# Two of four block sums by accumulating DMA, rows and activations parked in DRAM, and weight splitting ordered operation by operation, in an encoder layer

## The chip, the core and the metric

The kernel runs on one core of a Trainium2 chip. The metric is device time in microseconds; the profile is one execution of the program. TensorE multiplies, VectorE (DVE) and ScalarE (ACT) do the elementwise work, GpSimd (POOL) and SyncE (SP) issue the DMAs.

## What is computed

One encoder layer on 256 tokens of width 2048 in float32. The parts that matter here (constants filled in):

```python
h = layer_norm(x)
proj = h @ w_in                              # 2048 x 6144
...                                          # neighbourhood and differential attention
mixed = concat(na_out, diff_out) @ w_out     # 2048 x 2048
h = layer_norm(2**0.25 * h + mixed)
ffn = (silu(h @ w_gate) * (h @ w_up)) @ w_down   # 2048 x 5632 twice, 5632 x 2048
out = layer_norm(2**0.25 * h + ffn)
```

## The kernel before

**Products in three passes.** A float32 operand is split into a high part, rounded to the float32r type by a ScalarE copy (`split_hi`, line 336), and a low part, the difference, by a VectorE subtraction (`split_lo`, line 340). A product is three matmuls into one PSUM bank: high x high, high x low, low x high. Weights come as units of 128 rows by 1024 columns (`load`, line 326, on SP's queue) into the slab, a pool of 46 tiles of 4 KB for each partition, which also holds transposed activations and everything else of that size. Tokens are two tiles of 128.

**The units in order** (lines 307 to 322): six groups of the input projection, two of the output projection, the last 512 columns of gate and up together, ten groups of gate (`g`) and up (`u`) of 1024 columns each in turn, two groups of the down projection (`d`). Each group runs over its k tiles of 128 rows.

**Seven products.** In the `g` and `u` groups two neighbouring k tiles, two token tiles and two column halves make a 2 x 2 block product. `products` (line 931) lists seven products of 128 x 512 for four pairs of k tiles of a group (`SEVEN`, the pairs 0, 2, 4, 6) and eight for the four others. A seven pair needs sums of weight blocks. With r1 and r2 the two units, and columns in halves a and b, `seven_parts` (line 891) makes on VectorE: t1 = r1a + r1b and t3 = r1b + r2b in one tile, t2 = t1 + r2b and t4 = t2 + r2a in another; each tile is split as a whole, r1a by itself, and r2 as an ordinary unit. The products of sums 1 and 3 are the fourth and fifth, those of sums 2 and 4 the sixth and seventh. At a group's end VectorE joins the PSUM banks (`block_end`, line 1011); after a `u` group four tiles of middle activations are transposed on TensorE and copied to the slab by ScalarE (`mid_side`, line 866), where eleven tiles stay until the down projection; `mid_split` (line 874) splits them there. The residual rows `h` (four slab tiles) stay from the start to the end.

**The order of the queues.** The program is written out by a planner. `Timed` (line 60) keeps a clock for each engine and one for DMA from cost formulas (`note`, line 93) and when each tile is ready. The loop at line 1254 goes through the steps; a step in the `g` and `u` groups is one product. At each step it writes what must be there:

```python
window = order[i : i + (AHEAD_S if step.kind == "product" else AHEAD)]
for s in window[:URGENT]:          # URGENT = 3
    s.finish_parts()               # all that is left of these steps' weight work
```

then, up to eight times, elementwise side work, weight work of the steps in the window that the planner's clocks find ready while the clocks of ScalarE and VectorE are at most `SPARE` (2 us) ahead of TensorE's, and side work on TensorE. `finish_parts` (line 1223) writes a pair's whole list, and all products of a pair have that list. The engines then take their own instructions strictly in the written order. `Step.load` (line 1210) asks for weights `NPRE_S` units ahead. The planner's formulas used below:

```python
LATENCY = dict(pe=0.2, act=0.15, dve=0.13, pool=0.1, dma=1.2)              # line 61
start = self.clock[name] = max(self.clock[name], start) + (1.05 if name == "pool" else 0.1)
end = max(self.clock["dma"], start) + float(max(rows * dims[-1] * 4 / 360e3, rows * 0.0026))
if name == "pool": end += 2.0                                              # lines 102 to 105
cost = m / 2400 + 0.0135      # a matmul          (117)
cost = 0.1 + n / 1200         # ScalarE           (119)
cost = 0.07 + n / 960         # VectorE, two inputs (122)
```

Of the kernel before, what the change touches and what calls it, by code (L numbers as in the profile page):

```python
# [35 lines left out]
NSG = 5  # L36
SEVEN = (0, 2, 4, 6)


class Engine:  # L40
# [6 lines left out]
    def __getattr__(self, op):  # L47
        def call(*args, **kw):
            result = getattr(self.engine, op)(*args, **kw)  # L49
            outs, ins = [], []  # L50
            for i, (key, x) in enumerate([("", x) for x in args] + list(kw.items())):
                if hasattr(x, "tensor") and hasattr(x, "ap"):
                    (outs if key in ("out", "accum_out") or (i == 0 and not key) else ins).append(x)
            self.timed.note(self.name, op, outs, ins)
            return result

        return call
# [187 lines left out]
def layer_kernel(ctx: ExitStack, tc: tile.TileContext, A: dict, out: bass.AP):  # L245
# [6 lines left out]
    slab = ctx.enter_context(tc.tile_pool(name="slab", bufs=46))  # L252
# [8 lines left out]

    def slot(shape, dt=F32):
        return slab.tile(shape, dt, tag="slab", name=nm("sl"))
# [61 lines left out]

    def load(u):
        if u >= U:
            return
        r = slot([P, 1024])
# [14 lines left out]
    def split(u):  # L344
        if u not in wh:
            split_hi(u)
            split_lo(u)

    acc = {}

    def mm_step(t, u):
# [5 lines left out]
        xh = xh[:, t * P : (t + 1) * P]  # L357
        xl = xl[:, t * P : (t + 1) * P]
# [7 lines left out]
        nc.tensor.matmul(a1, xl, hi[:, 512:], start=False, stop=sp)  # L366

# [21 lines left out]
    AHEAD_S = 13  # L389
    NPRE = 7  # L390
    NPRE_S = 5
# [55 lines left out]
    def ln_side(key, t, g, b, store, tiles, n_whole):  # L447
# [10 lines left out]
        for c in range(4):  # L458
# [6 lines left out]
            if key == "1":  # L465
                if c not in hF:
# [39 lines left out]
    hF, forms = {}, {}  # L506

    def more_forms(i):
# [17 lines left out]
        parts = slot([P, 2, n, P], F32R)  # L526
# [339 lines left out]
    def mid_side(c, t, m):  # L866
        yield "pe", [m]
        bk = pe_transpose4(m)
        if c not in mid_whole:
            mid_whole[c] = slot([P, 4, S])  # L870
        nc.scalar.copy(mid_whole[c][:, :, t * P : (t + 1) * P], bk.rearrange("p (a b) -> p a b", b=P))
        have["mid whole", c] = have.get(("mid whole", c), 0) + 1

    def mid_split(c):

        if c not in mid_tiles:
            side.drain_until(lambda: have.get(("mid whole", c), 0) == 2)
            new_T(mid, mid_tiles, c)
            hi, lo = mid_tiles[c]
            nc.scalar.activation(hi, mid_whole[c], AF.Copy)  # L880
            nc.vector.tensor_tensor(lo, mid_whole[c], hi.bitcast(F32), op=ALU.subtract)
            have["mid", c, 0] = have["mid", c, 1] = 1
# [48 lines left out]
    def products(u):  # L931
# [13 lines left out]
        def t(n, m):  # L945
            return lambda: (sums[u]["hi"][n][:, m], sums[u]["lo"][n][:, m])

        a_, b_, c_, d_ = x(0, 0), x(1, 0), x(0, 1), x(1, 1)
        if i in SEVEN:
            def b11():  # L950
# [6 lines left out]
                (5, f(3), t(0, 0)),  # L957
                (7, f(0), t(0, 1)),
                (6, f(1), t(1, 0)),
                (4, d_, t(1, 1)),  # L960
# [14 lines left out]
    def take_product(u, n):  # L975
# [11 lines left out]
        nc.tensor.matmul(q[m], xl, yh, start=False, stop=stop)  # L987
        if not any(x in left for x in (1, 6, 7)) and 1 in q:
# [4 lines left out]
            nc.vector.tensor_tensor(vw[:, 0], q[7], e[:, 1], op=ALU.add)  # L993
            part["q1"], part["v"], part["vw"], part["w"] = e[:, 0], e[:, 1], vw[:, 0], vw[:, 1]
# [12 lines left out]
        elif stop and m == 4:  # L1007
            block_end(name, 1, 0, q[4], part["vw"], ALU.subtract)
            banks.give(q.pop(4))
# [311 lines left out]
```

## Time and profile before

| | us |
|---|---|
| median of 3 runs | 1149.44 (1146.36 to 1149.57) |
| the profiled execution | 1151.8 |
| its span, first to last instruction | 1150.0 |
| TensorE busy in the span | 1128.6 (98%) |
| VectorE busy | 855.2 (74%) |
| ScalarE busy | 572.3 (50%) |
| GpSimd busy | 43.2 (4%) |

Busy times are averages over stages with different limits, and a busy TensorE is not TensorE at its peak, since matmuls are pipelined: the number of matmuls in a stretch says more. All instructions carry the line of one helper (L49), so groups are told apart by the program's names: `sl` is a slab tile, `acc` a PSUM bank, `s`, `o` and `nb` are small rings of tiles. "a <-b" in a wait names the one that ended it. PEclk and the column behind the engines are the granted clock of TensorE as a share of full speed.

### The profile page before, as it was taken

To read this page: it belongs to the slowest core of one execution; us is meant where nothing else is said; L and a number is where in the kernel's file an instruction comes from. 1 tells how busy PE (TensorE), PEld (TensorE's weight loads), DVE (VectorE), ACT (ScalarE), POOL (GpSimd) and SP (SyncE) were. 2 spreads that over 40 slices of the span, in tenths; PEclk is the share of its full clock that TensorE was granted. 3 is DMA by queue.
4 is the path that set the end of the run, shared out by engine and by line. 5 is a ranking of instruction groups with operands and counts; after the bars stand their busy time and mean duration, and the time that the engine had idled before them with its cause. 6 is when DMAs were issued, how large, how long until landed. Compare 5 with 4: busy or idle time off the path is not lost.

```text
span 1150.0 us, 13909 instructions
## 1 busy us (share of the span) xinstructions
PE 1128.6 (98%) x5064; PEld 914.2 (79%) x5064; DVE 855.2 (74%) x1110; ACT 572.3 (50%) x740; POOL 43.2 (4%) x81
## 2 busy tenths in 40 slices
PE   9999999999999999999999999999999999999997
PEld 4788888888888858888778778778778888888885
DVE  7863866447784399989999989999989855455535
ACT  5552655426572155654654654555556544434420
POOL 2000002111000000000000000000000000000001
PEclk9999999999999999999999999999999999999999
DMA  9864548796676623656555556465556755577621
GB/s 329 268 187 151 154 148 184 189 216 157 163 255 204 235 91 115 213 187 203 195 185 196 170 188 234 128 220 183 170 196 223 269 194 174 177 232 246 217 79 73
DMA packets 64053, 218.51 MB, mean 190 GB/s; under 512 B 7669, under 2 KB 7797, under 8 KB 63985
## 3 DMA queue, kind: packets, MB, share of 16 engines
q1 hardware_dynamic: 61056, 209.74, 54.3%
q0 software_dynamic: 2768, 7.81, 5.0%
q8 instruction: 39, 0.64, 0.2%
q14 instruction: 30, 0.24, 0.1%
q10 hardware_dynamic: 160, 0.08, 0.0%
HBM read 215.50 MB, written 2.11 MB: 189 GB/s over the span
## 4 chain that ended last, share of the span: by engine, by line
PE 78%; DVE 13%; issue 3%; ACT 3%; DMA 1%; POOL 1%; POOLq 0%; ACTq 0%; DVEq 0%
PE acc L49 78%; DVE sl L49 10%; ACT sl L49 3%; DVE s L49 1%; DVE o L49 1%; ACT s L49 0%; DMA ident<-in_c_ident_dram 0%; DMA sl<-in_w_gate_dram 0%; DMA sl<-in_w_up_dram 0%; DVE stats L49 0%; POOL rstd L49 0%; POOL rs L49 0%; ACT o L49 0%; ACT L49 0%; POOLq L1317 0%
## 5 line engine op out<-in xcount | busy, mean ns | idle before, releaser
L49 PE MATMUL acc<-sl,sl 128*128 128x512 f32 (+1 forms) x4712 | 1076.7, 389 | 12.2 <-DVE o L49 5.5
L49 PEld LDWEIGHTS acc<-sl,sl 128*128 128x128 f32 x4712 | 869.5, 189 | 200.5 <-DVE sl L49 10.8
L49 DVE TENSOR_TENSOR sl<-sl,sl 128x1024 fp32r<-128x1024 f32 (+2 forms) x611 | 628.7, 1073 | 124.9 <-ACT sl L49 96.6
L49 ACT ACTIVATE sl<-sl 128x1024 fp32r<-128x1024 f32 (+1 forms) x491 | 473.2, 1011 | 297.1 <-DVE sl L49 167.5
L49 ACT ACTIVATE sl<-acc 128x256 fp32r<-128x256 f32 (+2 forms) x70 | 33.0, 499 | 102.4 <-PE acc L49 89.7
L49 DVE TENSOR_TENSOR sl<-acc,sl 128x256 fp32r<-128x256 f32 (+2 forms) x92 | 53.2, 593 | 33.4 <-ACT sl L49 32.6
L49 ACT COPY sl<-acc 128x512 f32<-128x512 f32 x50 | 28.2, 586 | 77.5 <-PE acc L49 77.4
L49 DVE SCALAR_TENSOR_TENSOR sl<-sl,acc 128x512 f32<-128x512 f32 x16 | 10.9, 679 | 58.1 <-PE acc L49 58.1
L49 DVE TENSOR_SCALAR sl<-acc 128x512 f32<-128x512 f32 x8 | 5.5, 688 | 37.2 <-PE acc L49 37.2
L49 DVE TENSOR_TENSOR sl<-sl 128x512 f32<-128x512 f32 x40 | 27.3, 683 | 0.0
L49 POOL DMA_DIRECT2D sl<-in_ln_g_dram x4 | 2.2, 560 | 652.2 <-DMA sl<-in_w_down_dram 596.7
L49 POOL DMA_DIRECT2D nb<-in_na_rpb_dram x32 | 19.6, 620 | 87.5 <-DVE s L49 87.5
L49 ACT ACTIVATE s<-s 128x512 f32<-128x512 f32 x20 | 12.3, 633 | 20.6 <-DVE s L49 20.6
L49 ACT ACTIVATE s<-s,mx 128x256 f32<-128x256 f32 x32 | 15.9, 500 | 12.5 <-DVE mx L49 12.5
L49 PEld LDWEIGHTS acc<-ident,s 128*128 128x128 f32 x136 | 17.1, 145 | 4.7 <-DVE o L49 0.9
L49 PE MATMUL acc<-ident,s 128*128 128x128 f32 x136 | 20.7, 281 | 0.1
L49 PEld LDWEIGHTS acc<-ident,sl 128*128 128x128 f32 x128 | 15.0, 140 | 7.0 <-issue 3.2
L49 DVE SCALAR_TENSOR_TENSOR sl<-sl,rstd,sl 128x512 f32<-128x512 f32 x22 | 16.5, 751 | 4.0 <-POOL rstd L49 3.1
L49 DVE BATCH_NORM_STATS2 stats<-sl 128x6 f32<-128x512 f32 x24 | 16.3, 690 | 3.0 <-DMA sl<-in_x_dram 2.4
L49 DVE SCALAR_TENSOR_TENSOR sl<-sl,mv,sl 128x512 f32<-128x512 f32 x24 | 17.7, 746 | 0.3
L49 PE MATMUL acc<-ident,sl 128*128 128x128 f32 x128 | 17.6, 273 | 0.1
L49 ACT ACTIVATE rows<-ident,rstd 128x128 f32<-128x128 f32 x1 | 0.4, 402 | 34.3 <-POOL rstd L49 34.3
(74 smaller groups left out, 198.9 us busy)
## 6 DMA issues: line engine op xcount, KB each, us to landing
sl<-in_w_in_dram SPq DMA_DIRECT2D x96, 512.0 KB, 4.9
sl<-in_w_down_dram SPq DMA_DIRECT2D x88, 512.0 KB, 4.3
sl<-in_w_gate_dram SPq DMA_DIRECT2D x80, 512.0 KB, 4.0
sl<-in_w_up_dram SPq DMA_DIRECT2D x80, 512.0 KB, 4.3
sl<-in_w_out_dram SPq DMA_DIRECT2D x32, 512.0 KB, 5.4
sl<-in_w_gate_dram SPq DMA_DIRECT2D x16, 256.0 KB, 4.0
sl<-in_w_up_dram SPq DMA_DIRECT2D x16, 256.0 KB, 4.2
sl<-in_x_dram SPq DMA_DIRECT2D x8, 256.0 KB, 5.0
```

Source lines behind the costliest of these rows:

```text
L49: result = getattr(self.engine, op)(*args, **kw)
```

## The change

- In a seven pair, sums 2 and 4 are made in the tile of sum 1, by two GpSimd DMAs that add a half of r2 from its slab tile (`accum_op`). Sum 2 is split before the second DMA. Sums 1 and 3 are made and split as before; sums 2 and 4 are split one by one into a tile each.
- The weight work is a list of single operations, each with its engine, what it reads and which of the list must come before (`op`, `seven_parts`, `one_parts`); `next_part` takes the first that is ready by the planner's clocks and whose engine's clock is at most `SPARE` ahead. `finish_parts` and `URGENT` are as before.
- The normalized residual rows go to DRAM after their transposes (eight GpSimd DMAs) and come back by four SP DMAs in the down projection's first group. The middle activations go to DRAM from a ring of two tiles (22 GpSimd DMAs) and come back one tile of four k tiles at a time (11 SP DMAs). Two of the sums' operand tiles for eight pairs share one slab tile.
- The planner is told which slab tiles are free (`leave`, `follows`). The window of steps `AHEAD_S` goes from 13 to 20, the weights asked for ahead, `NPRE_S`, from 5 to 8 units.

The diff, cut:

```diff
+    slots = dict(used=0, left=[])
     def slot(shape, dt=F32):
-        return slab.tile(shape, dt, tag="slab", name=nm("sl"))
+        t = slab.tile(shape, dt, tag="slab", name=nm("sl"))
+        if slots["used"] < SLOTS:
+            slots["used"] += 1
+        elif slots["left"]:
+            old = min(slots["left"], key=lambda x: nc.idle(x))
+            slots["left"].remove(old)
+            nc.follows(t, old)
+        return t
+    def leave(*tiles):
+        slots["left"] += tiles
     rings = {}
...
     raw, wh, wl = {}, {}, {}
+    h_d = dram.tile([2 * P, D], F32, name="h_d")
+    mid_d = dram.tile([NFC * P, 1024], F32, name="mid_d")
     def load(u):
         if u >= U:
             return
+        if u == U - KF - 10:
+            for t in range(2):
+                h[t] = [slot([P, 1024]) for _ in range(2)]
+                for i in range(2):
+                    nc.sync.dma_start(h[t][i], h_d[t * P : (t + 1) * P, i * 1024 : (i + 1) * 1024])
+        if units[u]["group"] == ("d", 0) and units[u]["k"] % 4 == 0:
+            c = units[u]["k"] // 4
+            side.drain_until(lambda: have.get(("mid whole", c), 0) == 2)
+            mid_whole[c] = slot([P, 2, 4, P])
+            nc.sync.dma_start(mid_whole[c], mid_d[c * P : (c + 1) * P, :])
...
     R0 = 3
     R1 = 8
     AHEAD = 7
-    AHEAD_S = 13
+    AHEAD_S = 20
     NPRE = 7
-    NPRE_S = 5
+    NPRE_S = 8
     stats, mv, rstd = {}, {}, {}
...
                 new_T(store, tiles, c)
             bk = pe_transpose4(chunk(h[t], c))
             if key == "1":
+                nc.gpsimd.dma_start(h_d[t * P : (t + 1) * P, c * 512 : (c + 1) * 512], chunk(h[t], c))
+                if c % 2:
+                    leave(h[t][c // 2])
                 if c not in hF:
                     hF[c] = slot([P, 4, S])
...
     def mid_side(c, t, m):
         yield "pe", [m]
         bk = pe_transpose4(m)
-        if c not in mid_whole:
-            mid_whole[c] = slot([P, 4, S])
-        nc.scalar.copy(mid_whole[c][:, :, t * P : (t + 1) * P], bk.rearrange("p (a b) -> p a b", b=P))
+        f = ring("nb", 2, (P, 512))
+        nc.scalar.copy(f, bk)
+        nc.gpsimd.dma_start(mid_d[c * P : (c + 1) * P, t * 512 : (t + 1) * 512], f)
         have["mid whole", c] = have.get(("mid whole", c), 0) + 1
-    def mid_split(c):
-        if c not in mid_tiles:
-            side.drain_until(lambda: have.get(("mid whole", c), 0) == 2)
-            new_T(mid, mid_tiles, c)
-            hi, lo = mid_tiles[c]
-            nc.scalar.activation(hi, mid_whole[c], AF.Copy)
-            nc.vector.tensor_tensor(lo, mid_whole[c], hi.bitcast(F32), op=ALU.subtract)
-            have["mid", c, 0] = have["mid", c, 1] = 1
+    def mid_hi(c):
+        hi, lo = mid_tiles[c] = slot([P, 2, 4, P], F32R), slot([P, 2, 4, P], F32R)
+        nc.scalar.activation(hi, mid_whole[c], AF.Copy)
+    def mid_lo(c):
+        hi, lo = mid_tiles[c]
+        nc.vector.tensor_tensor(lo, mid_whole[c], hi.bitcast(F32), op=ALU.subtract)
+        leave(mid_whole[c])
+        for i in range(4):
+            mid[4 * c + i] = hi[:, :, i, :], lo[:, :, i, :]
+        have["mid", c, 0] = have["mid", c, 1] = 1
...
+    def op(engine, fn, reads=(), after=()):
+        return dict(engine=engine, fn=fn, reads=reads, after=after, done=False)
+    def one_parts(u):
+        def lo():
+            split_lo(u)
+            leave(raw[u])
+        return [op("act", lambda: split_hi(u), lambda: [raw[u]]), op("dve", lo, lambda: [wh[u]], (0,))]
     def seven_parts(u):
         r1, r2 = raw[u], raw[u + 1]
-        def one():
-            sums[u] = dict(b11=slot([P, 2, 512], F32R), t=[slot([P, 2, 512]), slot([P, 2, 512])])
-            nc.scalar.activation(sums[u]["b11"][:, 0], r1[:, :512], AF.Copy)
-            nc.vector.tensor_tensor(sums[u]["t"][0][:, 0], r1[:, :512], r1[:, 512:], op=ALU.add)
-        def two():
-            split_hi(u + 1)
-            s = sums[u]
-            nc.vector.tensor_tensor(s["t"][0][:, 1], r1[:, 512:], r2[:, 512:], op=ALU.add)
+        s = sums[u] = {}
+        def t1():
+            s["t"] = slot([P, 2, 512])
+            nc.vector.tensor_tensor(s["t"][:, 0], r1[:, :512], r1[:, 512:], op=ALU.add)
+        def t3():
+            nc.vector.tensor_tensor(s["t"][:, 1], r1[:, 512:], r2[:, 512:], op=ALU.add)
+        def hi11():
+            s["b11"] = slot([P, 2, 512], F32R)
+            nc.scalar.activation(s["b11"][:, 0], r1[:, :512], AF.Copy)
+        def lo11():
             nc.vector.tensor_tensor(s["b11"][:, 1], r1[:, :512], s["b11"][:, 0].bitcast(F32), op=ALU.subtract)
-        def three():
-            split_lo(u + 1)
-            s = sums[u]
-            s["hi"] = [slot([P, 2, 512], F32R), slot([P, 2, 512], F32R)]
-            s["lo"] = [slot([P, 2, 512], F32R), slot([P, 2, 512], F32R)]
-            nc.scalar.activation(s["hi"][0], s["t"][0], AF.Copy)
-        def four():
-            s = sums[u]
-            a, b = s["t"]
-            nc.vector.tensor_tensor(b[:, 0], a[:, 0], r2[:, 512:], op=ALU.add)
-            nc.vector.tensor_tensor(b[:, 1], b[:, 0], r2[:, :512], op=ALU.add)
-            nc.scalar.activation(s["hi"][1], b, AF.Copy)
-            nc.vector.tensor_tensor(s["lo"][0], a, s["hi"][0].bitcast(F32), op=ALU.subtract)
-        def five():
-            s = sums[u]
-            nc.vector.tensor_tensor(s["lo"][1], s["t"][1], s["hi"][1].bitcast(F32), op=ALU.subtract)
-        return [([r1], one), ([r1, r2], two), ([r2], three), ([r2], four), ([r2], five)]
+            leave(r1)
+        def hi13():
+            s["hi"], s["lo"] = slot([P, 2, 512], F32R), slot([P, 2, 512], F32R)
+            nc.scalar.activation(s["hi"], s["t"], AF.Copy)
+        def lo13():
+            nc.vector.tensor_tensor(s["lo"], s["t"], s["hi"].bitcast(F32), op=ALU.subtract)
+        def add(col):
+            def to_t():
+                nc.gpsimd.dma_start(s["t"][:, 0], r2[:, col * 512 : col * 512 + 512], accum_op=ALU.add)
+            return to_t
+        def hi(n):
+            def f():
+                s[n] = slot([P, 2, 512], F32R)
+                nc.scalar.activation(s[n][:, 0], s["t"][:, 0], AF.Copy)
+            return f
+        def lo(n):
+            def f():
+                nc.vector.tensor_tensor(s[n][:, 1], s["t"][:, 0], s[n][:, 0].bitcast(F32), op=ALU.subtract)
+                if n == 4:
+                    leave(s["t"], r2)
+            return f
+        return [
+            op("dve", t1, lambda: [r1]),
+            op("dve", t3, lambda: [r1, r2]),
+            op("act", hi13, lambda: [s["t"]], (0, 1)),
+            op("act", hi11, lambda: [r1]),
+            op("dve", lo13, lambda: [s["hi"]], (2,)),
+            op("pool", add(1), lambda: [s["lo"]], (4,)),
+            op("dve", lo11, lambda: [s["b11"][:, 0]], (3,)),
+            op("act", lambda: split_hi(u + 1), lambda: [r2]),
+            op("dve", lambda: split_lo(u + 1), lambda: [wh[u + 1]], (7,)),
+            op("act", hi(2), lambda: [s["t"][:, 0]], (5,)),
+            op("dve", lo(2), lambda: [s[2][:, 0]], (9,)),
+            op("pool", add(0), lambda: [s[2][:, 1]], (10,)),
+            op("act", hi(4), lambda: [s["t"][:, 0]], (11,)),
+            op("dve", lo(4), lambda: [s[4][:, 0]], (12,)),
+        ]
...
                 stages[u] = seven_parts(u)
             else:
-                stages[u] = [([raw[u]], lambda: split(u))]
+                stages[u] = one_parts(u)
                 if units[u]["group"][0] == "d" and isinstance(units[u]["group"], tuple):
                     c = units[u]["k"] // 4
-                    if c not in mid_tiles:
-                        stages[u].insert(0, ([], lambda: mid_split(c)))
+                    if units[u]["group"][1] == 0 and units[u]["k"] % 4 == 0:
+                        stages[u] += [
+                            op("act", lambda: mid_hi(c), lambda: [mid_whole[c]]),
+                            op("dve", lambda: mid_lo(c), lambda: [mid_tiles[c][0]], (2,)),
+                        ]
         return stages[u]
+    def emit_part(o):
+        o["fn"]()
+        o["done"] = True
+    def next_part(coming, now):
+        for p in coming:
+            parts = prepare(*p)
+            for o in parts:
+                if o["done"] or not all(parts[i]["done"] for i in o["after"]):
+                    continue
+                clock = nc.clock[o["engine"]]
+                if clock <= now + SPARE and nc.ready(*o["reads"]()) <= max(clock, now):
+                    return o
+        return None
     class Step:
...
         def finish_parts(self):
             for p in self.parts:
-                todo = prepare(*p)
-                while todo:
-                    todo.pop(0)[1]()
+                for o in prepare(*p):
+                    if not o["done"]:
+                        emit_part(o)
...
         for _ in range(8):
             now = nc.clock["pe"]
             side.elementwise(now, BACKLOG)
-            for p in coming:
-                todo = prepare(*p)
-                while todo and nc.ready(*todo[0][0]) <= now and max(nc.clock["act"], nc.clock["dve"]) <= now + SPARE:
-                    todo.pop(0)[1]()
-                if todo:
-                    break
+            o = next_part(coming, now)
+            while o is not None:
+                emit_part(o)
+                o = next_part(coming, now)
             task, when = side.best()
             main = nc.ready(*step.operands()) if step.possible() else 1e9
```

## Rows read from the trace of the kernel before

**Rows 1.** The page, part 1: busy time, share of the span and instructions of each engine.
```profile
PE 1128.6 (98%) x5064; PEld 914.2 (79%) x5064; DVE 855.2 (74%) x1110; ACT 572.3 (50%) x740; POOL 43.2 (4%) x81
```

**Rows 2.** Windows: stretch, its length, busy us (instructions) by engine, granted clock, DMA share, GB/s.
```profile
600.00:650.00 50.00, 49.04 (x223) 40.11 (x223) 48.86 (x60) 28.17 (x34) 0.00 (x0) 1.00 0.57 199
...
850.00:900.00 50.00, 48.00 (x205) 38.65 (x204) 46.97 (x56) 27.92 (x34) 0.00 (x0) 0.97 0.67 238
...
950.00:1000.00 50.00, 50.00 (x223) 41.38 (x222) 24.99 (x21) 21.77 (x21) 0.00 (x0) 1.00 0.51 171
```

**Rows 3.** Windows: thirty-six periods of the stage, and a pause at a group's end.
```profile
496.14:888.98 392.84, 381.64 (x1673) 310.52 (x1672) 366.67 (x435) 222.44 (x262) 0.00 (x0) 0.99 0.57 193
...
723.20:727.00 3.80, 3.72 (x11) 3.02 (x12) 3.77 (x6) 0.01 (x1) 0.00 (x0) 0.55 0.00 0
```

**Rows 4.** Groups by form, 455:905: busy us, mean ns | idle before.
```profile
L49 DVE TENSOR_TENSOR sl<-sl,sl 128x1024 fp32r<-128x1024 f32 x207 | 246.7, 1219 | 15.1 <-ACT sl L49 13.7
L49 ACT ACTIVATE sl<-sl 128x1024 fp32r<-128x1024 f32 x206 | 209.4, 1053 | 132.8 <-DVE sl L49 113.2 <-PE acc L49 9.4 <-DMA sl<-in_w_gate_dram 5.3
L49 DVE TENSOR_TENSOR sl<-sl,sl 128x512 f32<-128x512 f32 x117 | 80.3, 687 | 5.4 <-DMA sl<-in_w_up_dram 2.9 <-DMA sl<-in_w_gate_dram 1.1
L49 DVE TENSOR_TENSOR sl<-sl,sl 128x512 fp32r<-128x512 f32 x39 | 26.7, 684 | 1.4 <-ACT sl L49 1.4
...
L49 ACT ACTIVATE sl<-sl 128x512 fp32r<-128x512 f32 x39 | 24.1, 617 | 0.0
...
L49 PE MATMUL acc<-ident,s 128*128 128x128 f32 x88 | 14.0, 286 | 0.1
```

**Rows 5.** Waits of TensorE and of ScalarE, 455:905: us in total, times, longest.
```profile
PE acc L49 <- DVE o L49: 5.5, 4, 1.8
PE acc L49 <- DVE sl L49: 3.5, 8, 0.8
PE acc L49 <- ACT sl L49: 2.1, 2, 1.2
...
ACT sl L49 <- DMA sl<-in_w_gate_dram: 5.3, 4, 2.9
ACT sl L49 <- DMA sl<-in_w_up_dram: 4.9, 3, 2.7
```

**Rows 6.** Timeline of two stretches: start, us, engine, operation [idle before <-releaser].
```profile
646.33 0.68 DVE L49 TENSOR_TENSOR sl<-sl 128x512 f32<-128x512 f32 x1
646.93 8.43 DVE L49 TENSOR_TENSOR sl<-sl,sl 128x512 f32<-128x512 f32 x9
...
714.70 0.56 ACT L49 COPY sl<-acc 128x512 f32<-128x512 f32 x1
715.30 1.42 DVE L49 TENSOR_TENSOR sl<-acc,sl 128x512 f32<-128x512 f32 x2 [0.52 <-ACT sl L49]
```

**Rows 7.** DMA issues: xcount, KB each, median us from issue to landing.
```profile
sl<-in_w_gate_dram SPq DMA_DIRECT2D x16, 256.0 KB, 4.0
...
sl<-in_ln_g_dram POOLq DMA_DIRECT2D x4, 512.0 KB, 4.6
sl<-in_ln_b_dram POOLq DMA_DIRECT2D x4, 512.0 KB, 7.0
out_dram<-sl SPq DMA_DIRECT2D x8, 256.0 KB, 2.1
```

**Rows 8.** Timeline of GpSimd, 330:1150.
```profile
411.65 0.75 POOL L49 TENSOR_SCALAR rstd<-mv 128x1 f32<-128x1 f32 x1 [8.16 <-DVE mv L49]
...
1009.75 0.60 POOL L49 DMA_DIRECT2D sl<-in_ln_g_dram  x1 [596.70 <-DMA sl<-in_w_down_dram]
```

**Rows 9.** Timeline of ScalarE, 888:906.
```profile
902.48 0.59 ACT L49 COPY sl<-acc 128x512 f32<-128x512 f32 x1 [0.72 <-PE acc L49]
...
903.93 0.58 ACT L49 COPY sl<-acc 128x512 f32<-128x512 f32 x1
904.74 0.59 ACT L49 COPY sl<-acc 128x512 f32<-128x512 f32 x1 [0.24 <-PE acc L49]
```

More of the change, by code (lines that the diff above doesn't have):

```diff
@@ L36 @@
 NSG = 5
+SLOTS = 46
 SEVEN = (0, 2, 4, 6)
@@ L53, in call @@
                     (outs if key in ("out", "accum_out") or (i == 0 and not key) else ins).append(x)
+            if "accum_op" in kw:
+                ins = ins + outs
             self.timed.note(self.name, op, outs, ins)
@@ L251, in layer_kernel @@
     tmp = ctx.enter_context(tc.tile_pool(name="tmp", bufs=2))
-    slab = ctx.enter_context(tc.tile_pool(name="slab", bufs=46))
+    slab = ctx.enter_context(tc.tile_pool(name="slab", bufs=SLOTS))
     dram = ctx.enter_context(tc.tile_pool(name="dram", bufs=1, space=bass.MemoryType.DRAM))
@@ L342, in split_lo, with tokens @@
         nc.vector.tensor_tensor(wl[u], raw[u], wh[u].bitcast(F32), op=ALU.subtract)
[L344 to L347, printed above, removed]
     acc = {}
+    def tokens(x, t):
+        return x[:, t] if len(x.shape) == 3 else x[:, t * P : (t + 1) * P]
     def mm_step(t, u):
@@ L356, in mm_step @@
         xh, xl = un["lhs"][un["k"]]
-        xh = xh[:, t * P : (t + 1) * P]
-        xl = xl[:, t * P : (t + 1) * P]
+        xh, xl = tokens(xh, t), tokens(xl, t)
         st, sp = un["first"], un["last"]
@@ L366, in mm_step @@
         nc.tensor.matmul(a1, xl, hi[:, 512:], start=False, stop=sp)
+        if t == 1:
+            leave(hi, lo)
     def mm_step32(t, u, lhs):
@@ L501, in part_split @@
         have[key, t, c] = 1
-    hF, forms = {}, {}
+    hF, forms, halves = {}, {}, []
     def more_forms(i):
@@ L525, in more_forms @@
         f = f[:, :n]
-        parts = slot([P, 2, n, P], F32R)
+        if n == 4:
+            parts = slot([P, 2, n, P], F32R)
+        elif len(halves) % 2 == 0:
+            halves.append(slot([P, 2, 2, 2, P], F32R))
+            parts = halves[-1][:, 0]
+        else:
+            parts = halves[-1][:, 1]
+            halves.append(None)
         yield "act", [f]
@@ new lines, in hi @@
+        def hi(n):
[6 more added lines that the diff above has]
+                nc.vector.tensor_tensor(s[n][:, 1], s["t"][:, 0], s[n][:, 0].bitcast(F32), op=ALU.subtract)
+                if n == 4:
+                    leave(s["t"], r2)
[16 more added lines that the diff above has]
+        ]
@@ L943, in b, with t13, t24 @@
             return lambda: w_block(u, row, col)
-        def t(n, m):
-            return lambda: (sums[u]["hi"][n][:, m], sums[u]["lo"][n][:, m])
+        def t13(m):
+            return lambda: (sums[u]["hi"][:, m], sums[u]["lo"][:, m])
+        def t24(n):
+            return lambda: (sums[u][n][:, 0], sums[u][n][:, 1])
         a_, b_, c_, d_ = x(0, 0), x(1, 0), x(0, 1), x(1, 1)
@@ L956, in products @@
                 (3, f(2), b(1, 1)),
[L957 to L960, printed above, removed]
+                (5, f(3), t13(0)),
+                (7, f(0), t13(1)),
+                (6, f(1), t24(2)),
+                (4, d_, t24(4)),
             ]
@@ L987, in take_product @@
         nc.tensor.matmul(q[m], xl, yh, start=False, stop=stop)
+        if n + 1 == len(products(u)):
+            s = sums.get(u)
+            leave(*([wh[u], wl[u]] if s is None else [s["b11"], s["hi"], s["lo"], s[2], s[4]]), wh[u + 1], wl[u + 1])
         if not any(x in left for x in (1, 6, 7)) and 1 in q:
@@ L993, in take_product @@
             nc.vector.tensor_tensor(vw[:, 0], q[7], e[:, 1], op=ALU.add)
+            part["tiles"] = e, vw
             part["q1"], part["v"], part["vw"], part["w"] = e[:, 0], e[:, 1], vw[:, 0], vw[:, 1]
@@ L1008, in take_product @@
             block_end(name, 1, 0, q[4], part["vw"], ALU.subtract)
+            leave(*part["tiles"])
             banks.give(q.pop(4))
@@ L1172, in last_steps @@
             for u in us:
-                xh, xl = (x[:, P:] for x in mid[units[u]["k"]])
+                xh, xl = (tokens(x, 1) for x in mid[units[u]["k"]])
                 nc.tensor.matmul(a, xh, wh[u][:, cols], start=False, stop=False)
@@ L1238, in operands @@
             t = self.t
-            return [wh[self.u], wl[self.u], *(x[:, t * P : (t + 1) * P] for x in un["lhs"][un["k"]])]
+            return [wh[self.u], wl[self.u], *(tokens(x, t) for x in un["lhs"][un["k"]])]
         def emit(self):
```

## The prediction

> **What bounds the kernel now.** I read the page's engine line first: TensorE 98%, VectorE 74% [rows 1]. A busy TensorE is not one at its peak, so the second view is the table by stretches. In the last projection (950 to 1000 us) TensorE is busy throughout and makes 223 matmuls in 50 us, 0.224 us each; in two stretches between 600 and 900 it makes 223 (short transposes among them) and 205, with VectorE at 49 and 47 of 50 us [rows 2]. That is the stage of the gate and up projections, with four pairs of k tiles by seven products and four by eight in each of ten groups; a seven and an eight pair together are called a period here, 15 products or 45 matmuls, 40 periods in all. I mark the stage by the first ScalarE copy of a group's end: nine groups, 36 periods, lie between 496.14 and 888.98 us, so **a period takes 392.84 / 36 = 10.91 us**, with VectorE busy for 366.67 / 36 = 10.19 us of it [rows 3]. TensorE's own need is 45 x 0.224 = 10.1 us and at most 14.0 / 40 = 0.35 us of transposes [rows 4]: about 10.4 us. So TensorE loses about 0.5 us a period, 20 us in the stage, and the waits say to whom: 9.0 of its 11.1 us wait for VectorE's outputs [rows 5]. They fall at the ends of groups, after which the clock is granted at 0.55 over 723.2 to 727 (1.0 before), a mean between the two levels of 1.2 and 2.4 GHz, so some more is lost [rows 3]. ScalarE waits 10.2 us for weights [rows 5]: tiles of the slab are short.
>
> **The sums by DMA.** Each seven pair loses two VectorE adds of 0.685 us, 80 in all; one 128x1024 subtraction (1.219 us) becomes two of 128x512 (2 x 0.684), and one 128x1024 ScalarE copy (1.053) two of 0.617 [rows 4]. Back to back the adds stand 0.60 us apart [rows 6], so VectorE's work in a period falls from 10.19 by 1.2 and rises by 0.1, to **9.1 us**. If that were all, TensorE would be the bound again. ScalarE gains 0.2 us a period, beside 222.44 / 36 = 6.2 us of work now [rows 3]: hidden. GpSimd issues 80 transfers at about 0.60 us each [rows 8] and has nothing else there.
>
> **When the transfers are waited for.** The order of each engine's queue is written by the planner, so I walk through its rule with its own constants (lines 61, 99 to 106, 117 to 122); they give the order only, and no time of mine. A step (one product) is 3 x 0.227 = 0.68 us. A seven pair's 14 operations come into the window of 20 steps 19 steps ahead of its first product, and all that are left are written 2 steps ahead of it (URGENT is 3, and all products of the pair share the list): 17 steps, 11.6 us. The longest path, with latencies: adds 1.33, hi13 1.10, lo13 1.27, transfer 1.05 + 0.73 + 2.0 + 1.2 = 4.98, hi2 0.68, lo2 0.73, transfer 4.98: 15.1 us before hi4 may start. So hi4 and lo4 are written into ScalarE's and VectorE's queues with the second transfer open. The next seven pair came into the window 15 steps after this one, 1.4 us before that; its two adds need 1.3 us, so its hi13 and lo13 stand **behind** the blocked hi4 and lo4. From then on each chain starts where the one before ends. Between two ends of chains the planner counts hi4, hi13, lo13, transfer, hi2, lo2, transfer: about 14.3 us, more than 10.2 of products, so this does not heal. The list is now forced 7 steps (4.8 us) after the end of the chain before, when the first transfer, due some 6.5 us after it, is open as well: hi2, lo2, the second transfer, hi4 and lo4 are written in one go. VectorE's queue reads per period: lo4, lo13, lo11, the low half of the second tile, the eight pair's two, two adds of the next pair, lo2, and lo4 again. The first transfer lies beside six operations; **between lo2 and lo4 VectorE has nothing**. Queued behind lo4 are the next pair's lo13 and the block ends, for which TensorE waits.
>
> **What that gap costs.** Idle from lo2 to lo4: the transfer D, hi4 0.62 [rows 4], and three hand-offs of at most 0.1 (a copy that starts at 714.70 for 0.56 is followed on VectorE at 715.30 [rows 6]). Then lo4 and hi13 run side by side, and lo13 waits for the longer hi13 (1.05) for 0.4 us. Together D + 1.3. No row shows an accumulating transfer between tiles, so D is bounded: below by a store of 256 KB at the end, 2.1 us from issue to landing; above by the second kind of GpSimd load, 7.0 us for 512 KB behind others. Between them are loads of 256 KB beside the weight stream, 4.0, and GpSimd loads of 512 KB, 4.6 [rows 7]. An accumulation reads 256 KB twice and writes it once, beside the same stream; I take **4.0**. Less than 2.1 I exclude: the store moves the same bytes once on quiet queues. The Trainium skill (DMA: Bandwidth & Descriptors, "Anatomy of one DMA — SWDGE (gpsimd) path") gives 2.0 us and bytes at 436 GB/s, by which 256 KB would take an estimated 2.6 us and the kernel about 1228 us; the GpSimd rows of [rows 7], at 4.6 and 7.0 us for 512 KB against 3.2 by that rule, stand above it.
>
> The period becomes 9.1 + 4.0 + 1.3 = 14.4 us: 3.5 more than 10.91. In 38 of 40 periods (the first ones still have the full window) that is 133 us. TensorE's pauses of some 4 us lower its clock, as after 723 [rows 3]; ten matmuls or so at half speed cost 2 us of 4 spare, so nothing further.
>
> **Middle activations through DRAM.** 22 stores of 256 KB on GpSimd's queue, 11 loads of 512 KB on SP's. The ScalarE copy goes to a ring of two buffers, so the third copy of a group's end waits for the first one's store: copies 2.3 us apart (902.48 to 904.74, with another between [rows 9]) against 0.6 + 2.1 us, so 0 to 2 us of ScalarE in five group ends, and those stores also queue behind a forced transfer that waits for lo2. ScalarE has the room: 0, at worst 10 us. The loads are emitted on SP eight units ahead of the stage's end and later every fourth unit; they add 1 in 8 to a stage in which TensorE is 100% busy and DMA half busy [rows 2]: 0. If SP waited for a slab tile there, the weights queued behind it would wait too; the freed tiles are the cover. The split of the middle activations is the same operations in another order.
>
> **Residual rows through DRAM.** Eight stores, GpSimd 8 x 0.60 us between the first LayerNorm and the stage. Four can stand ahead of the second token tile's rstd on GpSimd, which was idle for 8.16 us before that [rows 8], so 0, at worst 0.6 us. Four loads of 512 KB in the last projection: hidden as above.
>
> **More slab, longer look-ahead.** Parking frees up to 15 of 46 tiles. This takes away ScalarE's waits for weights, 10.2 us, and so at most 10 of the 20 us that TensorE loses [rows 5]. It is worth something only if VectorE is not held up; in the forecast it is 0.
>
> **Sum.** The profiled execution took 1151.8 us, 2.4 over the median. 1151.8 + 133 = 1285, and against the median **1282 us**. By D = 2.1 the period is 12.5, +60, 1210; by D = 5.3 it is 15.7, +182, 1331; at 7.0 the first transfer would outlast its six operations too and 1400 would be passed.
>
> **Rivals.** *The other side: faster, VectorE freed.* If the tail of the chain is written after enough other work (the planner finds hi2 ready before the list is forced, and work of the neighbouring pairs falls between lo2 and lo4), the transfers are hidden. It decides at a gap of 10.4 - 9.1 = 1.3 us a period: below that TensorE is the bound again, the period is 10.4, and 40 x 0.5 = 20 us are gained, 1129 us. For it: VectorE would be only 88% loaded, and the window is longer. Against: the chain's two transfers alone, at 4.0, and the operations between need 12 to 13 us of 11.6 in the window. *A part of the pairs exposed.* Group ends delay TensorE in the planner, so that in one period of two to four the first transfer has landed before the list is forced and some work falls into the gap: half of the 133 us, between 1170 and 1220. *Nothing measurable:* the gap eats just what the adds gave, D + 1.3 filled to 1.8 us; 1149. It needs a coincidence. That the change doesn't do what it says I see no way for: the two adds are gone from the list.
>
> **How the numbers follow.** Chances: forecast 0.62 (own range 1210 to 1331), part of the pairs 0.17, no change 0.05, faster 0.16. A measurement of this kernel can tell about 0.3% from no change. Slower by more 0.79, within 0.05, faster 0.16. The range leaves out the faster case and the transfers above 5.3 us: 1147 to 1335.
>
> **What would show it.** Right: between 460 and the stage's end TensorE's matmuls per 50 us fall to 150 to 175, VectorE's busy time to 31 to 34 of 50 us, and its longest waits are for ScalarE, with ScalarE's for the DMA of a slab tile onto itself, about 40 times 3 to 5 us, with hi4 right behind. The projections before and after keep their pace. Wrong: VectorE above 42 of 50 with TensorE at 220 matmuls (the gap is filled), or ScalarE's waits for that DMA under 1 us (D is short or hidden), or the loss outside the stage.

## The result: 1451 us, and the profile after

The changed kernel takes **1451.13 us** in the median (1443.55 to 1451.98) against 1149.21 of before on the same chip (one run more than in the table of before), a ratio of **1.262 [1.257, 1.267]**: 302 us slower. The page's engine line, to be held against [rows 1]:

```profile
PE 1235.1 (85%) x5064; PEld 965.0 (67%) x5064; DVE 807.3 (56%) x1070; ACT 578.3 (40%) x780; POOL 129.7 (9%) x191
```

VectorE has 48 us less to do, as meant, and yet every engine idles more. The table by stretches says where (columns as in [rows 2]); the third row spans nine groups of the stage, 36 periods, between ScalarE's first copies of a group's end:

```profile
500.00:550.00 50.00, 38.48 (x130) 28.46 (x131) 26.79 (x33) 19.30 (x25) 4.31 (x5) 0.80 0.51 142
700.00:750.00 50.00, 37.05 (x129) 27.78 (x128) 22.50 (x29) 17.56 (x22) 4.87 (x6) 0.80 0.57 158
...
518.57:1187.27 668.70, 483.76 (x1684) 359.88 (x1684) 329.04 (x403) 230.62 (x300) 70.97 (x88) 0.81 0.55 153
...
1250.00:1300.00 50.00, 50.00 (x222) 41.40 (x222) 22.92 (x20) 19.23 (x19) 0.00 (x0) 1.00 0.66 228
```

A period is 668.70 / 36 = **18.57 us** where it was 10.91 [rows 3]; VectorE works 329.04 / 36 = 9.14 us of it. 40 x 7.66 = 306 us: the whole loss lies in this stage. The last projection has 222 matmuls in 50 us, as before. The longest waits of VectorE, ScalarE and TensorE in the stage (470 to 1195; us in total, times, longest), where before had [rows 5]:

```profile
ACT sl L50 <- DMA sl<-sl: 377.9, 73, 9.5
DVE sl L50 <- ACT sl L50: 363.3, 79, 9.4
...
PE acc L50 <- ACT sl L50: 175.5, 49, 8.0
```

ScalarE waits for 73 of the 78 accumulating transfers issued there, 5.2 us each in the mean, and VectorE waits for ScalarE. Below, hi2 and lo2 are the split of sum 2 (hi2 the copy on ScalarE, lo2 the subtraction on VectorE), hi4 and lo4 that of sum 4, hi13 and lo13 that of the tile of sums 1 and 3, lo11 the low part of r1a. One pair and a half in the timeline (start, us, engine, operation [idle before <-releaser]):

```profile
699.70 0.86 POOL L50 DMA_DIRECT2D sl<-sl  x1 [12.93 <-DVE sl L50]
703.03 0.63 ACT L50 ACTIVATE sl<-sl 128x512 fp32r<-128x512 f32 x1 [4.99 <-DMA sl<-sl]
...
703.70 0.69 DVE L50 TENSOR_TENSOR sl<-sl,sl 128x512 fp32r<-128x512 f32 x1 [4.29 <-ACT sl L50]
...
704.68 0.86 POOL L50 DMA_DIRECT2D sl<-sl  x1 [4.12 <-DVE sl L50]
709.45 2.53 ACT L50 ACTIVATE sl<-sl 128x512 fp32r<-128x512 f32 x3 [5.79 <-DMA sl<-sl]
710.12 1.83 DVE L50 TENSOR_TENSOR sl<-sl,sl 128x512 fp32r<-128x512 f32 x2 [5.73 <-ACT sl L50]
...
710.14 13.68 PE L50 MATMUL acc<-sl,sl 128*128 128x512 f32 x45 [4.97 <-ACT sl L50]
...
716.32 0.86 POOL L50 DMA_DIRECT2D sl<-sl  x1 [10.77 <-DVE sl L50]
719.71 0.63 ACT L50 ACTIVATE sl<-sl 128x512 fp32r<-128x512 f32 x1 [3.95 <-DMA sl<-sl]
720.38 0.69 DVE L50 TENSOR_TENSOR sl<-sl,sl 128x512 fp32r<-128x512 f32 x1 [3.22 <-ACT sl L50]
```

The first transfer is issued at 699.70 and releases hi2 at 703.03, lo2 follows at 703.70; the second is issued at 704.68 and releases hi4 at 709.45, lo4 follows. **VectorE stands still for both**, 4.29 and 5.73 us. The prediction had it stand still for the second alone. The new transfers, and the parking beside them (count, KB, median us from issue to landing):

```profile
sl<-sl POOLq DMA_DIRECT2D x80, 256.0 KB, 3.5
...
mid_d<-nb POOLq DMA_DIRECT2D x22, 256.0 KB, 4.2
```

By their place in the pair, first transfers take 3.3 us in the median (mean 3.4), second ones 4.0 (mean 4.7).

What I had walked through by hand stands in the program: VectorE's instructions of one pair, in the order written (tiles by the kernel's own numbers; names at the right are mine):

```
517 TENSOR_TENSOR sl_802<-sl_781         128x512    t1
518 TENSOR_TENSOR sl_802<-sl_781,sl_782  128x512    t3
519 TENSOR_TENSOR sl_793<-sl_781,sl_793  128x512    lo11
520 TENSOR_TENSOR sl_805<-sl_782,sl_794  128x1024   low part of r2
521 TENSOR_TENSOR sl_807<-sl_802,sl_806  128x1024   lo13, frees the first transfer
522 TENSOR_TENSOR sl_808<-sl_784,sl_803  128x1024   low part of an eight pair's unit
523 TENSOR_TENSOR sl_811<-sl_802,sl_811  128x512    lo2, frees the second transfer
524 TENSOR_TENSOR sl_812<-sl_802,sl_812  128x512    lo4
525 TENSOR_TENSOR sl_815<-sl_785,sl_804  128x1024   low part of an eight pair's unit
```

Over all 40 pairs, six operations stand between lo13 and lo2 in 4, one in 26, none in 10; between lo2 and lo4 there are never any. I call a transfer bare when VectorE has at most one operation to do beside it.

### The profile page after: what moved, and what is told of

It is laid out like the page before. It is cut to its first block, busy times and chain, and to the rows that moved or that the text cites. A ratio compares the mean times of both kernels' runs of the same rounds, so it can differ in the third digit from the quotient of the medians.

```text
span 1448.6 us, 14144 instructions
## 1 busy us (share of the span) xinstructions
PE 1235.1 (85%) x5064; PEld 965.0 (67%) x5064; DVE 807.3 (56%) x1070; ACT 578.3 (40%) x780; POOL 129.7 (9%) x191
## 3 DMA queue, kind: packets, MB, share of 16 engines
q0 software_dynamic: 16688, 36.65, 14.4%
## 5 line engine op out<-in xcount | busy, mean ns | idle before, releaser
L50 PE MATMUL acc<-sl,sl 128*128 128x512 f32 (+1 forms) x4712 | 1186.1, 412 | 201.7 <-ACT sl L50 175.5
L50 PEld LDWEIGHTS acc<-sl,sl 128*128 128x128 f32 x4712 | 921.5, 201 | 447.0 <-ACT sl L50 198.6
L50 DVE TENSOR_TENSOR sl<-sl,sl 128x1024 fp32r<-128x1024 f32 (+2 forms) x571 | 584.2, 1064 | 466.2 <-ACT sl L50 417.1
L50 ACT ACTIVATE sl<-sl 128x1024 fp32r<-128x1024 f32 (+1 forms) x531 | 480.2, 951 | 593.8 <-DMA sl<-sl 383.1
L50 POOL DMA_DIRECT2D sl<-sl x80 | 69.1, 864 | 625.8 <-DVE sl L50 518.7
L50 ACT COPY sl<-acc 128x512 f32<-128x512 f32 x28 | 15.4, 591 | 31.3 <-PE acc L50 31.2
L50 ACT COPY nb<-acc 128x512 f32<-128x512 f32 x24 | 13.5, 581 | 25.9 <-PE acc L50 14.0
L50 POOL TENSOR_SCALAR rstd<-mv 128x1 f32<-128x1 f32 x6 | 3.4, 560 | 203.4 <-DVE mv L50 203.4
L50 POOL DMA_DIRECT2D mid_d<-nb x22 | 12.2, 559 | 80.0 <-ACT nb L50 79.9
```

## The experiments

Theory 1, formed from these rows: the engines take their queues in order, and each of the two transfers stands bare in them. Its rivals were the transfers' other effects, TensorE's low clock, and my own walk of the order. Periods below are worked out over 36 periods as above; the first expectations go by rougher readings of the changed kernel, 18.3 us a period with 9.3 of VectorE's work.

### Both transfers left out

```diff
-nc.gpsimd.dma_start(s["t"][:, 0], r2[:, col * 512 : col * 512 + 512], accum_op=ALU.add)
+nc.note("pool", "dma_start", [t], [x, t])     # the planner still counts it
```

> Leaves out the two accumulating transfers of each seven pair (sums 2 and 4 then equal sum 1), while the planner still counts them, so that every other instruction keeps its place in its queue. Theory 1, head-of-line: in the changed kernel VectorE works 9.3 us of an 18.3 us period and stands still 9.3 us because lo2 and lo4 wait through hi2 and hi4 for two transfers, with nothing between. Without them about 0.9 us each of hand-offs and copies stay: 9.3 + 1.8 = 11.1 us a period, total 1449 - 40 x 7.2 = 1160 us (1140 to 1185). Theory 2, the half clock of TensorE or the parking in DRAM carries the loss: the same order and the same parking keep the total above 1300 us.

1143.8 us, ratio 0.995 [0.993, 0.997]. The stage:

```profile
491.19:878.48 387.29, 379.70 (x1685) 309.43 (x1684) 323.20 (x403) 224.56 (x299) 8.63 (x16) 1.00 0.60 208
```

The period is 10.76 us and the clock 1.00 (0.81 with the transfers). Order, parking and window are the same, so **the 80 transfers make all of the loss**, 307 us, and the low clock is its consequence. The run also shows the prize: with VectorE down to 323.20 / 36 = 8.98 us a period and TensorE busy for 379.70 of 387.29 us, the period stays at 10.76, and in this order hidden transfers would have been worth 6 us.

### Transfers of 16 columns

```diff
-nc.gpsimd.dma_start(t, x, accum_op=ALU.add)
+nc.gpsimd.dma_start(t[:, :16], x[:, :16], accum_op=ALU.add)   # the planner counts 512 columns as before
```

> The two accumulating transfers move 16 columns in place of 512 (the sums are right in 16 columns only), in the same places of the queues. Theory 1 with a transfer that is mostly a fixed time: 2.0 to 2.5 us from issue to landing in place of 3.3 and 4.7, period 9.3 + 1.8 + 2 x 2.3 = 15.7 us, total 1449 - 40 x 2.6 = 1345 us (1310 to 1375). If the bytes beside the weight stream are what takes the time, it lands near the kernel without transfers, 1160 to 1200 us.

1362.7 us, ratio 1.185 [1.182, 1.189], as expected. With 1/32 of the bytes, (1362.7 - 1143.8) / 307 = 71% of the loss is left: most of it does not go with a transfer's own bytes. It is not all a fixed time either. First transfers took 2.1 us in the median, but second ones 3.9, longer than the 2.0 to 2.5 expected. Issue and landing times show the difference: 0.18 weight loads were in flight in the mean beside a first transfer and 0.74 beside a second, in the changed kernel 0.15 and 0.92.

### Each transfer alone

```diff
+if col == 1:     # e_no_first; col == 0 in f_no_second
+    nc.note("pool", "dma_start", [t], [x, t])
+else:
     nc.gpsimd.dma_start(t, x, accum_op=ALU.add)
```

> The change, with only the first of the two accumulating transfers of each seven pair left out (so the second sum is wrong by one block; the order in the queues is untouched). Theory 1 (each of the two transfers stands bare on the engines' queues, one after the other): ScalarE stood 4.7 to 5.8 us in front of the second sum's copy, so some 4.5 us a pair go, 40 pairs, 180 us: 1250 to 1295 us. Rival, my prediction's walk of the order (the first transfer lies beside six operations, only the second is bare): 1435 to 1455 us, nothing gained.

> The change, with only the second of the two transfers of each seven pair left out (so the fourth sum is wrong by one block; order untouched). Theory 1 (both bare): ScalarE stood 4.0 to 4.7 us in front of the fourth sum's copy, some 3.8 us a pair go, 40 pairs, 150 us: 1270 to 1310 us, and the two savings together, e_no_first's and this one's, come to the 307 us that leaving both out gave, within 40. Rival, my prediction's walk: all of the loss is the second's, 1140 to 1170 us.

Without the first 1262.95 us (1.098 [1.096, 1.101]); without the second 1217.8 us (1.058 [1.055, 1.062]). The stage of each, in that order:

```profile
502.30:1000.12 497.82, 422.55 (x1684) 322.69 (x1684) 325.74 (x403) 226.46 (x299) 39.78 (x52) 0.94 0.59 183
```

```profile
496.94:953.36 456.42, 409.03 (x1685) 317.92 (x1684) 324.86 (x404) 226.58 (x299) 39.80 (x52) 0.96 0.65 200
```

My prediction's walk falls: taking out the first transfer saved 188 us where the walk said nothing would be gained. The second's removal saved 233, more than the 140 to 180 expected, and the two savings sum to 421, not to 307 within 40. The idle time of VectorE explains the sum. Per period it is 18.57 - 9.14 = 9.43 us with both transfers, (497.82 - 325.74) / 36 = 4.78 with the second alone, (456.42 - 324.86) / 36 = 3.65 with the first alone, and 1.78 with none, when TensorE is the bound. The two single gaps come to 8.43 us, 1.0 short of the gap with both; the second transfers are shorter when alone (mean 3.5 us against 4.7). The savings sum to more than 307 for that reason, and because the last 1.78 us of a gap cost nothing: each single removal is counted from the full gap, both together only down to that floor.

### The sums back on VectorE, all else as changed

```diff
-nc.gpsimd.dma_start(s["t"][:, 0], r2[:, col * 512 : col * 512 + 512], accum_op=ALU.add)
+nc.vector.tensor_tensor(s["t"][:, 0], s["t"][:, 0], r2[:, col * 512 : col * 512 + 512], op=ALU.add)
...                                            # and "dve" for "pool" in the list of operations
```

> Only the two accumulating transfers are undone: VectorE makes sums 2 and 4 in the same tile; parking in DRAM, the order operation by operation, the wider window and the eight units ahead stay. Theory 1: the loss is gone; VectorE has 9.3 + 1.2 = 10.5 us of work a period against 10.4 of TensorE, total 1120 to 1160 us, about that of the kernel before. Theory 2, parking or the new order costs something by itself: above 1180 us.

1190.8 us, ratio 1.036 [1.034, 1.037]: theory 1 said 1120 to 1160 and missed. So the order costs something even without a DMA. Its forced tail (the end of a pair's list, which `finish_parts` writes in one go), in the timeline, and its stage below:

```profile
616.14 0.63 ACT L50 ACTIVATE sl<-sl 128x512 fp32r<-128x512 f32 x1 [2.26 <-DVE sl L50]
616.80 1.42 DVE L50 TENSOR_TENSOR sl<-sl,sl 128x512 fp32r<-128x512 f32 x2 [0.76 <-ACT sl L50]
618.31 2.53 ACT L50 ACTIVATE sl<-sl 128x512 fp32r<-128x512 f32 x3 [1.54 <-DVE sl L50]
618.98 1.83 DVE L50 TENSOR_TENSOR sl<-sl,sl 128x512 fp32r<-128x512 f32 x2 [0.76 <-ACT sl L50]
```

```profile
498.11:929.78 431.67, 402.07 (x1685) 317.98 (x1684) 375.37 (x474) 230.13 (x300) 8.60 (x16) 0.96 0.57 190
```

hi2, lo2 and the add, hi4, lo4 pass between the two engines with nothing beside them: VectorE loses 2 x 0.76 us a pair. Its work in the stage is 375.37 / 36 = 10.43 us a period; with 1.52 that makes 11.95, and the period is 431.67 / 36 = 11.99.

### Forcing only what is due

```diff
+DUE = [(3, 6), (7, 8), (7, 8), SUM13, SUM13, SUM2, SUM4]   # operations each product reads
-for o in prepare(*p):
-    if not o["done"]:
+for i, o in enumerate(prepare(*p)):
+    if not o["done"] and (self.due is None or i in self.due):
```

> All of the change stays, but a seven pair's weight work is no longer written whole two steps ahead of its first product: each step forces only what its own product reads (b11; the second unit; sums 1 and 3; sum 2; sum 4). Theory 1, it is the forced tail that closes the queues: the next pair's operations can go between lo2 and lo4, the period falls to 10.4 to 12.5 us, total 1130 to 1220 us. Rival: the chain of two transfers and five operations is too long for the window in any order, and the total stays above 1350 us.

> The kernel with both sums back on VectorE and only what a product needs forced ahead of it. The same sums on VectorE in the change's forced order took 1190.8 us, 41 above before. Theory 1 (those 41 us are hand-offs between ScalarE and VectorE of the forced tail, some 0.8 us each): 1130 to 1160 us, a period of 10.8 to 11.2 us. Rival (they come of adding in place in one tile, so that each sum waits for the difference before it): 1180 to 1195 us.

With the transfers: 1236.3 us, ratio 1.074 [1.072, 1.077], 16 above the expected range; 215 of the 302 us are won back. With VectorE's adds in their place: **1140.6 us, ratio 0.991 [0.988, 0.994]**, 50 less than in the forced order, so the loss of the run before was the forced tail's hand-offs, and not adding in one tile: VectorE's waits for ScalarE over the 36 periods go from 54.2 us (74 times) to 9.6 (12). This version is 0.9% faster than the kernel before. Its stage, and that of the transfers by the same rule of order:

```profile
493.92:874.70 380.78, 377.79 (x1690) 310.84 (x1689) 368.92 (x476) 228.88 (x300) 8.63 (x16) 1.00 0.64 216
```

```profile
510.21:976.55 466.34, 406.16 (x1690) 324.13 (x1689) 327.19 (x401) 226.86 (x299) 70.20 (x87) 0.93 0.76 217
```

A period takes 10.58 us with the sums on VectorE and 12.95 with them by DMA: 96 us for the kernel. In the order as written, 6 of 40 second transfers still have nothing behind them, and 5 have 2.4 us of VectorE's work.

### Work put behind the transfers

```diff
+EARLY = [(0, 13, (3, 0, 1, 2, 6, 4, 5, 7, 8)),   # up to the first transfer: 13 products ahead
+         (0, 4, (9, 10, 11)), (5, 2, (12, 13))]  # hi2, lo2, second transfer; hi4, lo4
+for n, lead, parts in EARLY:
+    for s in window[:lead]:
+        if s.kind == "product" and s.n == n and len(s.parts) == 1:
+            for i in parts:
+                o = prepare(*s.parts[0])[i]
+                if not o["done"]:
+                    emit_part(o)
 for s in window[:URGENT]:
```

`k_early` is this with what is due forced as above; `m_wide` has leads of 20, 8 and 2, and the planner's clocks no longer place parts 9 to 13.

> All of the change's work, both transfers too, in another order: a seven pair's operations up to the first transfer are written 13 products ahead of the pair's first product, the second sum's copy and difference and the second transfer 4 ahead, the fourth sum's 2 ahead of the product before its own, so that seven VectorE operations (6.2 us) stand between the first transfer and what waits for it and four (4.2 us) behind the second. Theory 1 (the loss is the order: transfers of 3.3 to 5.5 us with nothing beside them on VectorE): 1140 to 1190 us, a period of 10.8 to 11.8 us. Rival 2 (the transfers themselves slow the weights' loads or VectorE, wherever they stand): above 1215 us, near the 1236 us of forcing only what is due.

1246.1 us, ratio 1.083 [1.079, 1.086]: theory 1 missed again, by 56 us. The transfers had grown to 6.3 and 5.2 us in the mean, and counted over the whole queue, 15 of 40 pairs had only 2.4 us of VectorE's work behind the second, so this order did not give the cover that was meant. (The "seven of twenty-three" in the next expectation was a count over a part of the pairs.)

> All of the change's work in a still wider order: operations up to the first transfer 20 products ahead of the pair's first one, the second sum's copy and difference and the second transfer 8 ahead, the fourth sum's 7 products ahead of its own. In the written VectorE queue 4.3 us or more of work stand behind each first transfer and 4.5 us or more behind each second one, in every pair (in the order of k_early, which took 1246.1 us, seven of twenty-three pairs had only 2.4 us behind the second; there the transfers took 6.3 and 5.2 us). Theory 3 (what is left at 1236 and 1246 us is transfers that have less work beside them than they last): 1140 to 1190 us. Rival (the transfers share the DMA engines with the weights' loads: the more work is beside them, the longer they last, and the gain is eaten): 1200 to 1250 us with transfers of 5.5 us or more in the mean.

> The order of m_wide with both transfers left out (so the second and fourth sums lack a block each): what this order costs by itself. Theory 3 and its rival both: 1130 to 1155 us. If it comes out above 1180 us, the order itself (tiles held longer, differences ahead of the group's end) is a cost that neither had.

> The order of m_wide with both transfers cut to 16 of 512 columns (the sums lack the rest): the fixed part of a transfer stays, its bytes go. Theory 3: within 15 us of m_wide, since a transfer of 2 to 4 us and one of 4 to 5 us are both covered. Rival (bytes shared with the weights' loads): 1140 to 1165 us while m_wide stays above 1200 us.

1182.7 us (1.029 [1.027, 1.031]) with the transfers, 1159.3 (1.010 [1.008, 1.011]) without, 1159.1 (1.009 [1.007, 1.011]) with 16 columns. The three stages, in that order, then ScalarE's waits for the transfers in the first and the third (us in total, times, longest):

```profile
498.14:921.76 423.62, 396.63 (x1693) 316.27 (x1691) 328.30 (x401) 225.66 (x297) 70.28 (x87) 0.98 0.84 239
```

```profile
494.61:894.65 400.04, 384.24 (x1684) 311.42 (x1683) 327.12 (x402) 223.55 (x297) 8.67 (x16) 0.99 0.61 205
```

```profile
498.16:896.54 398.38, 382.00 (x1685) 309.12 (x1684) 328.29 (x401) 224.99 (x297) 70.29 (x87) 1.00 0.67 208
```

```profile
ACT sl L50 <- DMA sl<-sl: 91.8, 31, 5.6
...
ACT sl L50 <- DMA sl<-sl: 55.3, 27, 4.0
```

This is the test of the theory, and it holds: with some 4.2 us or more of VectorE's work behind every transfer but one (3.7), 80 transfers cost 23 us and not 307, and small ones, of 2.1 to 7.1 us, cost nothing at all. Most of a transfer is free once it is covered; what is left goes with its bytes. These 23 us are more than the 15 by which `m_wide_small` was expected to differ at most. They come from transfers that outlast their cover, not from slower weights: over the 36 periods no instruction of TensorE, VectorE or ScalarE waited for a weight load in either run, while ScalarE waited 36 us longer for the full transfers (4.7 us in the mean) than for the small ones (3.4), and VectorE 86.7 us for ScalarE against 56.2. The order itself cost 15 us against the first experiment, a little above what was expected.

### Is the wide window worth anything?

```diff
-AHEAD_S = 20
+AHEAD_S = 13
-NPRE_S = 8
+NPRE_S = 5
```

> The kernel that took 1140.6 us (both sums on VectorE, each step forcing only what its own product reads, rows and activations parked in DRAM), with the window of the kernel before: 13 products and 5 weight blocks ahead in place of 20 and 8. Parking makes room for the wide window; this run tells whether that room is worth anything. Theory 1, as my prediction put it (parking and the wider window are worth nothing): 1137 to 1144 us. Rival (the gain over before is the window's): 1146 to 1152 us.

1161.8 us, ratio 1.010 [1.009, 1.012], 21 us above the same kernel with the wide window, beyond either range. So the wide window and the longer look-ahead together are worth 21 us in that order, and carry it below the kernel before. Whether they need the room that parking makes was not tried.

## Why the prediction was wrong

The direction was right, by the mechanism named: an in-order queue that waits for an accumulating DMA. The time lies 116 us above the upper end. Step by step:

- **VectorE's work, 9.1 us a period.** 9.14. Right.
- **The walk of the order: failed.** I had the next pair's adds written ahead of the blocked tail, so that its lo13 would follow lo4 at once and lo11, the low halves and two adds would come behind lo13, beside the first transfer. In the written queue the adds come only after lo4, and lo11 and the low half of r2 stand ahead of lo13; six operations lie beside the first transfer in 4 pairs of 40. So there are **two gaps a pair, not one**. It is `SPARE` that holds the adds back: by the planner's own clocks, VectorE's stands 11 to 19 us ahead of TensorE's right after each of the 40 forced tails, where 2 are allowed, and the next pair's blocks are there already. No run tried another `SPARE`. (The 14.3 us between two ends of chains add up to 14.4; nothing hangs on it.)
- **The price of a gap, D + 1.3 with D = 4.0, 5.3 us.** The bare second one cost 4.78, with transfers of 3.5 us; D was 3.4 and 4.7 in the changed kernel. Right in size, though it is luck that 4.0 is the mean of the two: it was taken from loads out of DRAM. With this very price, two gaps less the one operation that mostly stands in the first, the period is 9.1 + 2 x 5.3 - 1.2 = 18.5 us, against 18.57 measured. The count was the error, not the price. The Trainium skill (DMA: Bandwidth & Descriptors, "Anatomy of one DMA — SWDGE (gpsimd) path") gives 2.0 us and bytes at 436 GB/s, by which 256 KB would add an estimated 0.6 us. The 2.1 us of 16 columns agrees with the first part; the 256 KB add 1.2 us here (3.3 us in the median, with few weight loads beside the transfer).
- **The range.** It covered D from 2.1 to 5.3 and the gap closing, but I put no bound on how many transfers stand bare, though the walk behind that number had the most steps. Both bare is some 1438 us by the same sum over 38 periods; that case was given no chance at all.
- **TensorE's low clock costs nothing further.** Right: in the 36 periods VectorE's work and its waits for ScalarE, 329.04 + 330.5 of 668.70 us, fill the time at a clock of 0.81, and ScalarE in turn waited for TensorE's products for only 18.6 us (waits over 518.57:1187.27: us in total, times, longest):

```profile
DVE sl L50 <- ACT sl L50: 330.5, 73, 9.3
...
ACT sl L50 <- PE acc L50: 18.6, 4, 5.1
ACT nb L50 <- DMA mid_d<-nb: 11.2, 4, 4.1
```

- **Parking at nothing.** By itself it costs nothing that shows: the first experiment has all of its stores and loads, and takes 1143.8 us. In the changed kernel ScalarE did wait 11.2 us for parking stores (the last row above), about the 10 us put as the worst case; without the transfers the stage has no such wait, so it is a part of their loss. **The wider window at nothing** was put so for a VectorE that is held up, and could show nothing under the two gaps; the bound given otherwise, at most 10 us, was too low, since the wide window was worth 21 us in the order with VectorE's adds.
- **Rivals.** The faster one, 1129 us, is not reached by any order tried: in the best covered one the transfers' bytes still cost 23 us, more than the 6 us that the freed VectorE was worth in the first experiment. "A part of the pairs" looked the wrong way: for fewer gaps than one a pair, not for more.
- **What would show it.** I gave 150 to 175 matmuls in 50 us, VectorE 31 to 34 busy, some 40 waits of 3 to 5 us. It was 129 or 130, 22 to 27, and 73 of 5.2: nearly twice the waits, a little longer. The projections kept their pace.

## What to carry to other kernels

When an operation is given to a DMA, its whole latency falls on every engine that waits for it with nothing else to do, so count in the written queue, for each transfer, how much work lies between what releases it and what waits for it: mostly 0 to 1.2 us here made 80 transfers cost 307 us, some 4.2 us or more made them cost 23. Leave out the transfers alone first: that gives the most that hiding them can bring in that order (6 us here) before any order is built for it. Forcing only what the next product reads, in the wide window, with all sums on VectorE, took 1140.6 us, less than the 1143.8 with the transfers left out; what hidden transfers would bring in that order was not run.

## What the runs showed of the hardware

- An accumulating transfer of 256 KB between slab tiles takes at least 3.2 us from issue to landing, one of 8 KB at least 2.1. It grows with the weights' loads in flight beside it, worked out from issue and landing times of `m_wide`: 3.3 us in the mean with less than half a load in flight (13 transfers), 4.3 with 0.5 to 1.5 (41), 6.1 with 1.5 or more (26). VectorE's work beside it does not lengthen it: those 13 took 3.32 us with VectorE busy for 85% of their time, and the 42 with less than half a load in the changed kernel 3.35 us with VectorE busy for 21%.
- GpSimd is occupied longer by its issue (0.863 us) than by that of a plain store (0.558); groups by form of the changed kernel, 500 to 850:

```profile
L50 POOL DMA_DIRECT2D sl<-sl x38 | 32.8, 863 | 292.6 <-DVE sl L50 238.1 <-PE acc L50 43.5 <-issue 10.9
L50 POOL DMA_DIRECT2D mid_d<-nb x8 | 4.4, 558 | 23.5 <-ACT nb L50 23.5
```

- With TensorE standing still for ScalarE's outputs 45 times in the 36 periods, 3.5 us in the mean, it was granted 0.81 of its clock over the stage, a mean between its levels of 1.2 and 2.4 GHz; with the transfers gone it was 1.00.
